# A decoder block on one core: feed-forward products as three of 256 columns, with breaks of 64-column products between them

## The chip, the core and the metric

The kernel runs on one core of a Trainium2 chip. Its time is the device time of one execution in microseconds (us). The kernel before took 2075.42, 2079.7 and 2075.45 us in three runs, a median of 2075.45 us.

## What is computed

A decoder block over 256 tokens of width 2048, in float32: a SwiGLU feed-forward of width 5632, a token mixer (8 heads of a gated delta rule and 16 heads of a state space model that share one input and one output projection), a second feed-forward, and a gated embedding with a last normalisation.

```python
h = h + 0.5 * swiglu(rmsnorm(h, ffn1_norm), ffn1_w_gate, ffn1_w_up, ffn1_w_down)
proj = rmsnorm(h, mix_norm) @ w_in
...
h = h + jnp.concatenate([o_gdn, o_ssm], axis=-1) @ w_out
h = h + 0.5 * swiglu(rmsnorm(h, ffn2_norm), ffn2_w_gate, ffn2_w_up, ffn2_w_down)
gate = jax.nn.sigmoid(rmsnorm(h, ple_norm) @ ple_w_gate)
h = h + gate * rmsnorm(p @ ple_w_proj, ple_post_norm)
return rmsnorm(h, final_norm)
```

## The kernel before

Everything is kept transposed: 128 channels on the partitions, the 256 tokens as columns. Nearly all of the work is weight tiles of 128 x 128 times an operand of 256 columns. To keep float32 accuracy both sides are split into two parts, hi (rounded) and lo (the rest): a weight tile w and an operand slice x give hi(w) hi(x), hi(w) lo(x) and lo(w) hi(x). The split operands lie in SBUF as `xs` (the block's state, 16 slices), `hid` (half of the feed-forward's hidden width, 22 slices) and `osp` (the mixer's output, 16 slices); each slice has its hi and its lo half side by side, 512 columns. The weights come by SP's queue into `raw`; for each piece of 1024 columns (8 slices) ScalarE casts `hi` (L118) and VectorE subtracts `lo` (L119).

A step is one weight tile with one slice. There are two ways to take it. `chain` (L122 to L133) multiplies hi(w) with hi and lo of the slice in one product of 512 columns into both halves of a PSUM bank (L130), and lo(w) with the hi half in a product of 256 columns into the first half (L128, or L132 in the first step). The bank's halves are added when the tile is done: `total_of` copies one half out by ScalarE (L168) and adds the other by VectorE (L169). `single` (L135 to L149) takes three products of 256 columns, all into the first half (L145 to L147), and its caller reads that half alone.

`product` uses `chain`: all gate, up and down tiles of both feed-forwards (`ffn`, from L318 on; per feed-forward two halves of 22 gate and 22 up tiles with `xs`, then 16 down tiles with `hid`), the first two tiles of the mixer's input projection, and all but the last tile of the embedding's gate. `embed` calls `chain` itself with `psp`. `single` serves the rest of the input projection, the output projection with `osp`, and the last tile.

`stats` makes the row of a normalisation: products of one column (L240) and, after VectorE and GpSimd, two products of 128 columns that spread the row over the partitions (L249), which `use` then reads. It and `embed` and the mixer's heads are generators: `tick`, called after each piece of a tile, advances each of them by one part, so their small products stand in between the big ones. The order within an engine is that of a scheduler with a simulated timeline.

The PSUM tiles `mm` (four banks) hold tiles of products; `mx_bank` gives one of four other banks for the small products. `ones` is a 128 x 128 tile of ones.

Of the kernel before, what the change touches and what calls it, by code (L numbers as in the profile page):

```python
# [12 lines left out]
ALU = mybir.AluOpType  # L13
# [37 lines left out]
STEP = 3  # L51
WARM = 11
AHEAD = 0


def constant_pack():
# [12 lines left out]
def tile_hybrid_block(ctx, tc, xT, pT, con, par, wgu1, wd1, wnar, win, wout, wgu2, wd2, wproj, wple, outT):  # L69
    nc = tc.nc  # L70
    act, dve, pool, pe = nc.scalar, nc.vector, nc.gpsimd, nc.tensor
# [14 lines left out]
    ones = cp.tile([P, P], F32, name="ones")  # L86
# [17 lines left out]
    def mx_bank(name):  # L104
        return psx.tile([P, 512], F32, tag="mx", name=name)
# [16 lines left out]
    def chain(ps, hi, lo, act_in, ks, first=True, last=True):  # L122


        for i, (w, k) in enumerate(ks):
            start, stop = first and i == 0, last and i == len(ks) - 1
            if not start:
                pe.matmul(ps[:, 0, :], lo[:, w, :], act_in[:, k, 0, :], start=False, stop=False,  # L128
                          skip_group_check=True)
            pe.matmul(ps, hi[:, w, :], act_in[:, k], start=start, stop=stop, skip_group_check=True)  # L130
            if start:
                pe.matmul(ps[:, 0, :], lo[:, w, :], act_in[:, k, 0, :], start=False, stop=False,  # L132
                          skip_group_check=True)  # L133

    def single(src, act_in, ks):  # L135

# [29 lines left out]

    def total_of(ps, out):
        act.copy(out, ps[:, 0, :])  # L168
        dve.tensor_tensor(out=out, in0=out, in1=ps[:, 1, :], op=ALU.add)  # L169


    side = []
# [1 line left out]
    def tick():  # L174
        for g in list(side):
            with tc.high_priority(offset=AHEAD):
                if next(g, g) is g:
# [53 lines left out]
    def stats(squares, width, name, use, wait=2):  # L231


        for _ in range(wait):
            yield
        m = small.tile([P, 2], F32, tag="rm", name=name + "m")
        banks = [mx_bank(f"{name}{c}") for c in range(2)]
        for i, sq in enumerate(squares):
            for c, ps in enumerate(banks):
                pe.matmul(ps[:, 0:1], sq[:, c * P:(c + 1) * P], ones[:, 0:1], start=i == 0,  # L240
                          stop=i == len(squares) - 1)
        for c, ps in enumerate(banks):
            dve.tensor_scalar(m[:, c:c + 1], ps[:, 0:1], 1.0 / width, EPS, op0=ALU.mult, op1=ALU.add)
        y = rsq(m, 2, name)
        if wait:
            yield
        ps = mx_bank(name + "row")
        for c in range(2):
            pe.matmul(ps[:, c * P:(c + 1) * P], y[:, c:c + 1].to_broadcast([P, P]), ident, start=True, stop=True)  # L249
        use(ps[:, :T])  # L250

    def begin(gen):
        side.append(gen)
        return gen
# [5 lines left out]
    def new_acc():  # L260
        return tp.tile([P, 2, T], F32, tag="acc", name="acc")
# [10 lines left out]
    ps = mx_bank("warm")  # L272
# [35 lines left out]
    def token_stats(use):  # L308

        acc = new_acc()  # L310
        for k in range(0, KD, 4):
            yield
            for i in (k, k + 2):
                sumsq(acc, hT[:, i:i + 2, :], i == 0)
        yield from stats(fold(acc), D, "ffn", use)


    def ffn(wgu, wd, squares, next_name, start=None):  # L318

        with tc.tile_pool(name="hid", bufs=1) as hp, tc.tile_pool(name="ft", bufs=2) as ft:  # L320
            hid = hp.tile([P, HF, 2, T], F32R, name="hid")
            r = hp.tile([P, T], F32, name="r")
            rh = hp.tile([P, T], F32, name="rh")
            new = new_acc()

            def use(row):
                dve.tensor_copy(r, row)
                act.mul(rh, row, 0.5)

            gen, held = None, []  # L330
            for half in range(2):
                for f in range(0, HF, 2):
                    t = ft.tile([P, 2, T], F32, tag="t", name="t")
                    s = ft.tile([P, 2, T], F32, tag="s", name="s")
                    tiles = [(wgu[half * HF + f + j, b], out[:, j, :]) for j in range(2) for b, out in ((0, t), (1, s))]
                    if start is not None:
                        start([out for _, out in tiles[:3]])
                        tiles = tiles[3:]
                        start = None
                    for n, (w, out) in enumerate(tiles):  # L340
                        if gen is None and (n == len(tiles) - 2 or len(tiles) == 1):
                            gen = begin(stats(squares(), D, "ffn", use) if squares else token_stats(use))
                        product([w], xs, full, out)
                    held.append((f, t, s))

                    if len(held) == 1 and squares is None and half == 0 and f == 0:
                        continue
                    drain([gen])
                    for g, t, s in held:
                        dve.tensor_tensor(out=t, in0=t, in1=over(r, 2), op=ALU.mult)  # L350
                        act.activation(t, t, AF.Silu)
                        dve.tensor_tensor(out=s, in0=s, in1=t, op=ALU.mult)
                        split_into(hid[:, g:g + 2], s)
                    held.clear()
                for o in range(0, KD, 2):
                    t = ft.tile([P, 2, T], F32, tag="t", name="t")
                    for j in range(2):
                        product([wd[half, o + j, q] for q in range(2)], hid, list(range(HF)), t[:, j, :])
                    dve.tensor_tensor(out=t, in0=t, in1=over(rh, 2), op=ALU.mult)
                    dve.tensor_tensor(out=hT[:, o:o + 2, :], in0=hT[:, o:o + 2, :], in1=t, op=ALU.add)  # L360
                    if half == 1:
                        split_x(o, next_name)
                        split_x(o + 1, next_name)
                        sumsq(new, hT[:, o:o + 2, :], o == 0)
        return new
# [5 lines left out]
    with ExitStack() as mix:  # L371
# [34 lines left out]
        ps = mm_bank("nar")  # L406
# [498 lines left out]
        op = mix.enter_context(tc.tile_pool(name="op", bufs=1))  # L905
# [8 lines left out]

        acc2 = new_acc()
        order = list(range(8, 16)) + list(range(8))
        for o in range(0, KD, 2):
            for j in range(2):
                ps = single(wout[o + j], osp, order)
                dve.tensor_tensor(out=hT[:, o + j, :], in0=hT[:, o + j, :], in1=ps, op=ALU.add)  # L920
            split_x(o, "ffn2")
            split_x(o + 1, "ffn2")
            sumsq(acc2, hT[:, o:o + 2, :], o == 0)
# [30 lines left out]
    with tc.tile_pool(name="f2", bufs=2) as f2:  # L954
# [29 lines left out]
            act.mul(pp[:, o, :], hT[:, o, :], pv("final")[:, o:o + 1])  # L984

        for o in range(0, KD, 2):
            last = o == KD - 2
            t = f2.tile([P, 2, T], F32, tag="t", name="t")
            for j, n in ((0, 1), (1, 1)) if last else ((0, 2),):
# [117 lines left out]
```

## Time and profile before

| | |
|---|---|
| median of three runs | 2075.45 us |
| the profiled execution's own time | 2079.58 us |
| span of its instructions | 2077.7 us |
| mean granted TensorE clock | 0.995 of full speed |
| TensorE products busy | 2051.2 us, 99%, 12882 products |
| VectorE busy | 1366.0 us, 66% |
| ScalarE busy | 1034.8 us, 50% |
| GpSimd busy | 175.3 us, 8% |
| DMA | 384.58 MB, mean 185 GB/s |

Matmuls are pipelined: a product's time in the profile runs from its start to a modelled end, and the next one starts before that. So the pace is read from start to start, in the timeline, or from the number of products in a window. A float32 product of the small kind (operands that aren't split) shows as two records in the profile.

### The profile page before, as it was taken

Reading aid. Unit: us, or ns where it says so; the run is one execution under the profiler, and the core shown is the slowest. Engines: PE = TensorE matmul, PEld = TensorE weight load, DVE = VectorE, ACT = ScalarE, POOL = GpSimd, SP = SyncE. Lnnn points to the kernel's source line nnn. Section 1 sums busy time; section 2 is a strip of 40 time slices with the busy share of each in tenths; the row PEclk is TensorE's granted clock in tenths of the full one; section 3 lists DMA queues with packets and bytes.
Section 4 is the critical chain, followed back from the end, with each engine's and each line's share of the span. In section 5 each row is a group of like instructions: output and inputs, shape, how many; then the busy total and the mean of one; then the engine's idle time right before and its main releaser. Section 6 shows DMA issues by size and latency. Waiting matters only on the chain.

```text
span 2077.7 us, 31523 instructions
## 1 busy us (share of the span) xinstructions
PE 2051.2 (99%) x12882; PEld 1835.2 (88%) x12882; DVE 1366.0 (66%) x2063; ACT 1034.8 (50%) x1544; POOL 175.3 (8%) x206
## 2 busy tenths in 40 slices
PE   9999999999999999989999999999999999999997
PEld 7888888888888889989999998888888888888886
DVE  7665555556555669999887666556555565556675
ACT  6544444444444555645545456444444444445554
POOL 2000000000000013303321111000000000000011
PEclk9999999999999999999999999999999999999998
DMA  7555455655555666544444555555556555545652
GB/s 271 185 183 185 176 176 187 210 184 188 193 173 179 203 223 205 184 160 164 174 165 161 190 183 184 193 191 183 163 186 211 190 183 183 186 164 189 210 183 102
DMA packets 64481, 384.58 MB, mean 185 GB/s; under 512 B 7744, under 2 KB 9280, under 8 KB 31184
## 3 DMA queue, kind: packets, MB, share of 16 engines
q1 hardware_dynamic: 61600, 376.76, 52.6%
q0 software_dynamic: 2448, 5.28, 0.8%
q8 instruction: 101, 1.65, 0.3%
q10 hardware_dynamic: 288, 0.52, 0.1%
q14 instruction: 44, 0.36, 0.0%
HBM read 377.78 MB, written 4.75 MB: 184 GB/s over the span
## 4 chain that ended last, share of the span: by engine, by line
PE 91%; DVE 2%; DMA 2%; issue 2%; POOL 1%; ACT 1%; POOLq 0%; DVEq 0%; ACTq 0%; SPq 0%
PE mm L130 50%; PE mm L128 24%; PE mm L146 4%; PE mm L147 4%; PE mm L145 4%; PE mm L132 1%; DMA hT<-rows 1%; DVE lo L119 1%; DMA blky<-Z 1%; DMA Y<-blky 1%; PE ip L694 0%; PE pj L130 0%; DVE u L566 0%; PE iy L694 0%; POOL hT L829 0%
## 5 line engine op out<-in xcount | busy, mean ns | idle before, releaser
L119 DVE TENSOR_TENSOR lo<-raw,hi 128x1024 fp32r<-128x1024 f32 (+1 forms) x774 | 858.5, 1117 | 482.6 <-ACT hi L118 481.8
L130 PE MATMUL mm<-xs,hi 128*128 128x512 f32 x3088 | 1078.2, 397 | 0.0
L118 ACT CAST hi<-raw 128x1024 fp32r<-128x1024 f32 (+1 forms) x774 | 744.4, 963 | 567.9 <-PE mm L130 372.7
L128 PE MATMUL mm<-xs,lo 128*128 128x256 f32 x2895 | 812.8, 281 | 3.2 <-DVE lo L119 3.2
L130 PEld LDWEIGHTS mm<-xs,hi 128*128 128x128 f32 x3088 | 568.2, 188 | 123.2 <-ACT hi L118 0.3
L128 PEld LDWEIGHTS mm<-xs,lo 128*128 128x128 f32 x2895 | 543.6, 188 | 14.8 <-DVE lo L119 4.9
L130 PE MATMUL mm<-hid,hi 128*128 128x512 f32 x1408 | 492.5, 397 | 0.0
L128 PE MATMUL mm<-hid,lo 128*128 128x256 f32 x1344 | 377.8, 281 | 0.0
L130 PEld LDWEIGHTS mm<-hid,hi 128*128 128x128 f32 x1408 | 260.2, 188 | 59.0
L128 PEld LDWEIGHTS mm<-hid,lo 128*128 128x128 f32 x1344 | 253.3, 188 | 3.0
L147 PE MATMUL mm<-xs,lo 128*128 128x256 f32 x816 | 229.9, 282 | 4.3 <-DVE lo L119 4.3
L145 PE MATMUL mm<-xs,hi 128*128 128x256 f32 x816 | 230.1, 282 | 0.0
L146 PE MATMUL mm<-xs,hi 128*128 128x256 f32 x816 | 229.5, 281 | 0.0
L147 PEld LDWEIGHTS mm<-xs,lo 128*128 128x128 f32 x816 | 154.9, 190 | 5.0 <-DVE lo L119 4.9
L146 PEld LDWEIGHTS mm<-xs,hi 128*128 128x128 f32 x816 | 154.9, 190 | 0.4
L145 PEld LDWEIGHTS mm<-xs,hi 128*128 128x128 f32 x816 | 154.7, 190 | 0.6 <-issue 0.3
L168 ACT COPY t<-mm 128x256 f32<-128x256 f32 x167 | 62.3, 373 | 161.9 <-PE mm L130 160.7
L205 POOL TENSOR_TENSOR acc<-acc,sq 128x512 f32<-128x512 f32 x43 | 63.1, 1467 | 944.8 <-ACT sq L204 906.3
L169 DVE TENSOR_TENSOR t<-t,mm 128x256 f32<-128x256 f32 x167 | 69.9, 418 | 86.9 <-ACT t L168 86.8
L168 ACT COPY s<-mm 128x256 f32<-128x256 f32 x88 | 32.8, 373 | 149.0 <-PE mm L130 148.9
L169 DVE TENSOR_TENSOR s<-s,mm 128x256 f32<-128x256 f32 x88 | 37.1, 422 | 74.0 <-ACT s L168 73.9
L147 PE MATMUL mm<-osp,lo 128*128 128x256 f32 x256 | 71.8, 281 | 0.0
(303 smaller groups left out, 1452.8 us busy)
## 6 DMA issues: line engine op xcount, KB each, us to landing
raw<-in_wgu SPq DMA_DIRECT2D x173, 1024.0 KB, 4.8
raw<-in_wd SPq DMA_DIRECT2D x128, 704.0 KB, 4.1
raw<-in_win SPq DMA_DIRECT2D x52, 1024.0 KB, 4.8
raw<-in_wout SPq DMA_DIRECT2D x16, 1024.0 KB, 4.8
raw<-in_wple SPq DMA_DIRECT2D x16, 1024.0 KB, 4.8
first<-in_wgu SPq DMA_DIRECT2D x11, 256.0 KB, 6.7
hold<-hT POOLq DMA_DIRECT2D x4, 512.0 KB, 4.0
Lb<-blkl SPq DMA_DIRECT2D x4, 512.0 KB, 4.6
```

Of the source, the lines that this page charges most:

```text
L118: act.copy(hi, src)
L119: dve.tensor_tensor(out=lo, in0=src, in1=hi.bitcast(F32), op=ALU.subtract)
L128: pe.matmul(ps[:, 0, :], lo[:, w, :], act_in[:, k, 0, :], start=False, stop=False, skip_group_check=True)
L130: pe.matmul(ps, hi[:, w, :], act_in[:, k], start=start, stop=stop, skip_group_check=True)
L132: pe.matmul(ps[:, 0, :], lo[:, w, :], act_in[:, k, 0, :], start=False, stop=False, skip_group_check=True)
L145: pe.matmul(ps[:, 0, :], hi[:, i, :], act_in[:, k, 0, :], start=k == ks[0], stop=False)
L146: pe.matmul(ps[:, 0, :], hi[:, i, :], act_in[:, k, 1, :], start=False, stop=False)
L147: pe.matmul(ps[:, 0, :], lo[:, i, :], act_in[:, k, 0, :], start=False, stop=k == ks[-1])
L168: act.copy(out, ps[:, 0, :])
L169: dve.tensor_tensor(out=out, in0=out, in1=ps[:, 1, :], op=ALU.add)
L205: pool.tensor_tensor(out=acc, in0=acc, in1=sq, op=ALU.add)
```

## The change

`chain` now takes a step as `single` does, in three products of 256 columns into the bank's first half, and `total_of` only copies that half. A new function `pause` issues four products of 64 columns, float32, ones times ones, into columns 256 to 319 of a bank; nobody reads them. It is called in `stats` behind the row's products (not for the last row), in both feed-forwards ahead of every fourth pair of gate and up tiles (f = 4, 12, 20 of each half), ahead of the down tiles and in the middle of them, ahead of the output projection, and ahead of the third pair of embedding gate tiles.

```diff
+PAUSE = 4
+WIDTH = 64
...
         for i, (w, k) in enumerate(ks):
             start, stop = first and i == 0, last and i == len(ks) - 1
-            if not start:
-                pe.matmul(ps[:, 0, :], lo[:, w, :], act_in[:, k, 0, :], start=False, stop=False,
-                          skip_group_check=True)
-            pe.matmul(ps, hi[:, w, :], act_in[:, k], start=start, stop=stop, skip_group_check=True)
-            if start:
-                pe.matmul(ps[:, 0, :], lo[:, w, :], act_in[:, k, 0, :], start=False, stop=False,
-                          skip_group_check=True)
+            pe.matmul(ps[:, 0, :], hi[:, w, :], act_in[:, k, 0, :], start=start, stop=False)
+            pe.matmul(ps[:, 0, :], hi[:, w, :], act_in[:, k, 1, :], start=False, stop=False)
+            pe.matmul(ps[:, 0, :], lo[:, w, :], act_in[:, k, 0, :], start=False, stop=stop)
+
+    def pause(ps):
+
+        for i in range(PAUSE):
+            pe.matmul(ps[:, 256:256 + WIDTH], ones, ones[:, 0:WIDTH], start=True, stop=True)
...
     def total_of(ps, out):
         act.copy(out, ps[:, 0, :])
-        dve.tensor_tensor(out=out, in0=out, in1=ps[:, 1, :], op=ALU.add)
...
             pe.matmul(ps[:, c * P:(c + 1) * P], y[:, c:c + 1].to_broadcast([P, P]), ident, start=True, stop=True)
+        if wait:
+            pause(ps)
         use(ps[:, :T])
...
                 for f in range(0, HF, 2):
+                    if f % 8 == 4:
+                        pause(mx_bank("calm"))
...
+                pause(mx_bank("calm"))
                 for o in range(0, KD, 2):
+                    if o == 8:
+                        pause(mx_bank("calm"))
...
         order = list(range(8, 16)) + list(range(8))
+        pause(mx_bank("calm"))
         for o in range(0, KD, 2):
...
         for o in range(0, KD, 2):
+            if o == 4:
+                pause(mx_bank("calm"))
```

TensorE's order where the first feed-forward goes from its last up tile (`xs`) to its first down tile (`hid`), before and after; the numbers behind the names tell one buffer from the next:

```order
L128 MATMUL mm_2243<-xs_80,lo_2267 128x256
L130 MATMUL mm_2243<-xs_80,hi_2266 128x512
L130 MATMUL mm_2294<-hid_111,hi_2297 128x512
L132 MATMUL mm_2294<-hid_111,lo_2298 128x256
L128 MATMUL mm_2294<-hid_111,lo_2298 128x256
```

```order
L129 MATMUL mm_2907<-xs_80,hi_2938 128x256
L130 MATMUL mm_2907<-xs_80,hi_2938 128x256
L131 MATMUL mm_2907<-xs_80,lo_2939 128x256
L136 MATMUL calm_2972<-ones_83 128x64 x4
L129 MATMUL mm_2978<-hid_111,hi_2981 128x256
L130 MATMUL mm_2978<-hid_111,hi_2981 128x256
L131 MATMUL mm_2978<-hid_111,lo_2982 128x256
```

Two products to a step have become three, and the break stands between the two kinds of tiles, where the source has it.

TensorE's order where the mixer's last projection tile (`xs`) is followed by the first tile of the output projection (`osp`), before and after:

```order
L145 MATMUL mm_11236<-xs_80,hi_11267 128x256
L146 MATMUL mm_11236<-xs_80,hi_11267 128x256
L147 MATMUL mm_11236<-xs_80,lo_11268 128x256
L145 MATMUL mm_11302<-osp_11159,hi_11305 128x256
L146 MATMUL mm_11302<-osp_11159,hi_11305 128x256
L147 MATMUL mm_11302<-osp_11159,lo_11306 128x256
```

```order
L148 MATMUL mm_13324<-xs_80,hi_13355 128x256
L149 MATMUL mm_13324<-xs_80,hi_13355 128x256
L150 MATMUL mm_13324<-xs_80,lo_13356 128x256
L136 MATMUL calm_13390<-ones_83 128x64 x4
L148 MATMUL mm_13395<-osp_13247,hi_13398 128x256
L149 MATMUL mm_13395<-osp_13247,hi_13398 128x256
L150 MATMUL mm_13395<-osp_13247,lo_13399 128x256
```

The products of `single` are the same as before, three lines further down; the break is all that is new there.

## Rows read from the trace of the kernel before

**Rows 1.** The page: TensorE's busy time, and the granted clock in 40 slices

```profile
PE 2051.2 (99%) x12882; PEld 1835.2 (88%) x12882; DVE 1366.0 (66%) x2063; ACT 1034.8 (50%) x1544; POOL 175.3 (8%) x206
...
PEclk9999999999999999999999999999999999999998
```

**Rows 2.** The page's costly groups: count, busy us, mean ns; idle before, releaser

```profile
L130 PE MATMUL mm<-xs,hi 128*128 128x512 f32 x3088 | 1078.2, 397 | 0.0
...
L128 PE MATMUL mm<-xs,lo 128*128 128x256 f32 x2895 | 812.8, 281 | 3.2 <-DVE lo L119 3.2
...
L130 PE MATMUL mm<-hid,hi 128*128 128x512 f32 x1408 | 492.5, 397 | 0.0
...
L147 PE MATMUL mm<-xs,lo 128*128 128x256 f32 x816 | 229.9, 282 | 4.3 <-DVE lo L119 4.3
...
L169 DVE TENSOR_TENSOR t<-t,mm 128x256 f32<-128x256 f32 x167 | 69.9, 418 | 86.9 <-ACT t L168 86.8
...
L169 DVE TENSOR_TENSOR s<-s,mm 128x256 f32<-128x256 f32 x88 | 37.1, 422 | 74.0 <-ACT s L168 73.9
```

**Rows 3.** TensorE's timeline, an up tile: start us, duration us

```profile
200.08 0.40 PE L130 MATMUL mm<-xs,hi 128*128 128x512 f32 x1
...
203.26 0.40 PE L130 MATMUL mm<-xs,hi 128*128 128x512 f32 x1
```

**Rows 4.** TensorE's timeline, a down tile

```profile
1901.63 0.40 PE L130 MATMUL mm<-hid,hi 128*128 128x512 f32 x1
...
1905.86 0.39 PE L130 MATMUL mm<-hid,hi 128*128 128x512 f32 x1
```

**Rows 5.** Windows of TensorE: us, busy us (count), granted clock, DMA share, GB/s

```profile
783.10:806.50 23.40, 23.40 (x209) 1.00 0.56 196
...
1125.00:1205.00 80.00, 80.00 (x679) 1.00 0.55 190
```

**Rows 6.** TensorE's timeline, the kernel's last tile and what follows it

```profile
2057.38 0.28 PE L145 MATMUL mm<-xs,hi 128*128 128x256 f32 x1
...
2063.03 0.50 PE L240 MATMUL final<-ones,acc 128*128 128x1 f32 x4
```

**Rows 7.** TensorE's timeline around the mixer's row of statistics

```profile
777.29 0.60 PE L249 MATMUL mixrow<-cont,mix 128*128 128x128 f32 x4
...
778.21 0.28 PE L146 MATMUL mm<-xs,hi 128*128 128x256 f32 x1
...
779.15 0.28 PE L145 MATMUL mm<-xs,hi 128*128 128x256 f32 x1
```

**Rows 8.** TensorE's timeline around four 64-column products in the mixer

```profile
924.25 1.00 PE L694 MATMUL ip<-oT,LA 128*128 128x64 f32 x8
925.06 0.36 PE L145 MATMUL mm<-xs,hi 128*128 128x256 f32 x1
...
926.19 0.28 PE L145 MATMUL mm<-xs,hi 128*128 128x256 f32 x1
...
928.57 0.28 PE L145 MATMUL mm<-xs,hi 128*128 128x256 f32 x1
```

**Rows 9.** TensorE's timeline behind other 64-column products

```profile
1082.42 1.06 PE L694 MATMUL iy<-Y,blockQ 128*128 128x64 f32 x8
...
1083.84 0.28 PE L145 MATMUL mm<-xs,hi 128*128 128x256 f32 x1
...
1084.20 0.28 PE L145 MATMUL mm<-xs,hi 128*128 128x256 f32 x1
```

**Rows 10.** TensorE's timeline from the mixer's last projection tile into the output projection

```profile
1123.00 0.28 PE L147 MATMUL mm<-xs,lo 128*128 128x256 f32 x1
...
1123.45 0.28 PE L145 MATMUL mm<-osp,hi 128*128 128x256 f32 x1
...
1124.39 0.28 PE L147 MATMUL mm<-osp,lo 128*128 128x256 f32 x1
```

**Rows 11.** A window of all engines: PE, PEld, DVE, ACT, POOL, granted clock, DMA

```profile
900.00:950.00 50.00, 46.48 (x374) 45.88 (x373) 43.91 (x128) 22.24 (x40) 8.79 (x15) 0.93 0.45 155
```

## The prediction

> **What bounds the kernel now.** I read the page first: TensorE is busy for 99% of the span at the full granted clock [rows 1], so the time is TensorE's instruction stream and little else. The table of costly groups says what the stream is: products of 512 and 256 columns by the thousand, with next to no idle time in front of them: the lo products with xs waited 3.2 us in total in `chain`, and 4.3 in `single` [rows 2]. VectorE, ScalarE and the DMA rows are cover: what the change takes from them is worth nothing by itself. So the question is at what pace TensorE goes through its columns, and for that I went to the timeline and to windows.
>
> There are two paces at the same granted clock. A feed-forward step of `chain` (512 and 256 columns) with xs goes from 200.08 to 203.26 us in nine steps: 353.3 ns a step, or 117.8 ns for 256 columns [rows 3]. With hid it is 12 steps in 4.23 us, 352.5 ns, 117.5 for 256 columns [rows 4]. In the mixer, `single` does the same step as three products of 256, and there 783.10 to 806.50 holds 209 of them; each is 0.28 us long, so two or three of the count only reach in, and 23.40 us over 206.5 is 113.3 ns. The output projection, the same instructions with osp, took 80 us for 679 less the same 2.5: 118.3 ns [rows 5]. The last tile of the kernel, three products with xs behind a `chain`, took 5.65 us for 48: 117.7 ns [rows 6]. So three products instead of two are no faster as such. Some stretches run at 113.3 and others at 117.5 to 118.3, and I call the two paces fast and slow.
>
> What changes the pace is another kind of product in between. Behind the two 128-column products of the mixer's row of statistics, the fast pace became slow: 779.15 less 778.21 is 0.94 us for eight [rows 7]. Behind four 64-column products (two records each, eight in the row) it is fast: from 926.19 to 928.57 stand 21 products, 113.3 ns each [rows 8]. There are four such breaks in the mixer, and all four left it fast; two had found it slow. Once, behind sixteen mixed records of 64 columns, it was slow afterwards: 1083.84 to 1084.20 is 0.36 for three [rows 9]. Without a break I find no product with xs at which the fast pace was lost.
>
> **The change part by part.** (a) `chain` becomes three products of 256. By rows 3 and 6 this costs nothing in the slow pace with xs (353.3 against 3 x 117.7 = 353.1). It is what makes the feed-forward stream the same as the one that ran fast. There are 3088 steps with xs and 1408 with hid [rows 2].
>
> (b) The 255 VectorE adds of `total_of` go (69.9 + 37.1 us, [rows 2]). TensorE, ACT and the queues wait for none of them where it counts: the products behind them had no idle time. I take 0; at the drained ends of a stage it could give back some tenths of a microsecond.
>
> (c) The breaks. The built order has 29 of them, each four 64-column products, where the source puts them. The nearest row is the one of the mixer: from 924.25 to 926.19 there are a break and nine steps at 113.3 (1.02 us), which leaves 0.92 us for the break [rows 8]. Its eight records alone are 0.81 (924.25 to 925.06), the floor. A ceiling of 1.0 allows for more settling. 29 x 0.92 = 26.7 us, all on the path, since TensorE has nothing else that waits; between 23.5 and 29. Of their waits the built order has only ones for TensorE's own earlier products (the break before in that bank), so nothing new holds up the products queued behind. Where a break sits behind a row of statistics (seven of the 29) VectorE's reading of the row comes up to 0.9 us later, and TensorE has a tile of products in front of the next thing that needs it.
>
> (d) The fast pace where it is reached. Counted in the built order, 7765 products with xs follow a break with no hid or osp in between (354 stand ahead of the first break). At 117.8 - 113.3 = 4.5 ns each that is -34.9 us. The other 1223 products with xs come behind hid or osp without a break; the nearest row, the last tile, says that a slow stream stays slow, so 0, with -5.5 as the other bound.
>
> (e) The products with hid: 4224 of them, each run behind a break, and 768 with osp. The trace has no break ahead of hid or osp. What it has is the entry: the fast pace of xs (1123.00 to 1123.45, four in 0.45) turned slow at the very first product with osp, with no idle time, and the next eight took 0.94 us [rows 10]; it stayed there for 80 us [rows 5]. I read this as belonging to the operand and take slow, at the pace of osp since that is the same instruction: (118.3 - 117.5) x 4224 = +3.4 us. Bounds: 0, and if they go fast like xs, -4.2 x 4224 = -17.7, and osp -5.0 x 768 = -3.8.
>
> The sum: 26.7 - 34.9 + 3.4 = -4.8 us. The profiled execution took 2079.58 us (span 2077.7 and 1.9 around it), so it would be 2074.8 there. That execution lies 4.1 over the median of the three runs, 2075.45, two of which agree at 2075.4; on the median it is **2070.6 us**, 0.23% less.
>
> The Trainium skill ("TensorE: Matmul & The Clock Gate", section on the back-to-back issue gap) gives a warm product N/2.4 GHz plus about 2.5 ns, fixed. By that rule a third product per step costs 4496 x 2.5 = 11.2 us, an estimate from that page, and speaks against (a). The sum would then be 2081.8 us. With xs the trace doesn't agree: 512 and 256 columns took 353.3 ns and three of 256 took 353.1 [rows 3, 6], and neither pace is the page's 109 ns for 256 columns.
>
> **The rivals.**
> 1. *hid and osp go fast too.* For it: the break sets the pace in every stretch where I can see one, and neither operand ever had a break ahead of it, so one entry from xs is thin evidence. Against: that entry, without any stall. Then 26.7 - 34.9 - 17.7 - 3.8 - 5.5 = -35.2: 2040.2 us.
> 2. *The fast pace doesn't last in the feed-forward.* The longest stretch that I can lean on is some 206 products [rows 5]; here nine runs with xs have 576 to 768 products between breaks, beside DMAs, casts and subtractions for every 24. If it is lost after 206, only 2899 of the 7765 run fast, 13.0 us, and 26.7 + 3.4 - 13.0 = +17.1: 2092.6 us, slower. It decides from the length at which the gain covers 30.1 us: 6690 products, about 627 in each long run. Against it: the stalls in the mixer (4.3 us in front of `single`'s lo products, [rows 2]) left fast products behind them.
> 3. *The breaks don't set the pace here*, as in rows 7 and 9, where products of 64 or 128 columns left it slow; then the change is its price alone, +30.1: 2105.6 us. For it: each of those breaks had other operands than a break here, and with a fixed rhythm one bad outcome would repeat at all 29 places. Against: the nearest form left it fast four times of four.
> 4. *The third product of a step costs its own time in the feed-forward.* With osp three products of the slow pace take 3 x 118.3 = 354.9 ns, with hid two take 352.5 [rows 4, 5]. If the 2.4 ns are the third product's and not osp's, as (e) has it for hid, the 3088 steps with xs pay them too: +7.4 us, 2078.0 us. Against it: rows 3 and 6, where xs shows no such difference.
>
> Beside these the mixer's order shifts a little, and its dip in the granted clock (0.93 over the 50 us from 900, which at half clock is 7 us at half speed, 3.5 us lost, [rows 11]) may move, go or get a second: 3.5 us up or down, which I put into the range of the forecast.
>
> **How the numbers follow.** Chances: forecast 0.48, hid and osp fast 0.27, fast pace lost 0.14, breaks without effect 0.08, a price for the third product 0.03. The forecast's own range is -34.9 + 23.5 - 5.5 = -16.9 to -34.9 + 29 + 3.4 = -2.5, with 3.5 for the dip: 2055 to 2077. A measurement of this kernel can tell about 0.2%, 4.2 us, from no change, so the line for faster is at 2071.3. In the forecast's case I give 0.70 to faster, 0.25 to the same and 0.05 to slower. Faster: 0.27 + 0.34 = 0.61; the same: 0.12, and 0.03 for rival 2 where the pace lasts about 600 products: 0.15; slower: 0.24. The range goes down to rival 1 with the floor price of the breaks (2040.2 - 3.2 = 2037, with a little of the dip: 2036) and up to rival 2 (2093); rival 3 is left out.
>
> **What would show it.** In the profile after, a window between two breaks of the gate and up tiles has 113.3 ns for each product (100 us hold 883 of them, where slow gives 849), and the down tiles about 118. A break's eight records take 0.8 us. If windows of the down tiles show 113, rival 1 is right and the time is near 2040. If the count falls from 883 to 849 within a run, rival 2 is right; if the window right behind a break has 849, rival 3. The forecast is wrong in its cause, whatever the time, if the pace changes at places that aren't breaks or changes of operand.

## The result, and the profile after

The changed kernel took 2106.99 us (median of four runs, 2103.44 to 2110.08) against 2076.89 beside it: 1.45% slower, the ratio of the times is 1.0145 with a 95% interval of 1.0132 to 1.0158. The forecast was 2070.6 with a range of 2036 to 2093, so the sign was wrong and the time lies outside the range. It is the time of rival 3, 2105.6. The profiled execution took 2105.64 us (span 2103.8), 26.1 more than that of before; the medians differ by 30.1, since that execution of before lies 2.7 us over the median beside it and that of after 1.4 under its own.

The page of the changed kernel, TensorE's line and the granted clock in 40 slices, answers to [rows 1]:

```profile
PE 2076.6 (99%) x17642; PEld 2068.6 (98%) x17642; DVE 1256.5 (60%) x1790; ACT 1026.2 (49%) x1544; POOL 172.7 (8%) x206
...
PEclk9999999999999999999999999999999999999998
```

TensorE is as full as before, at the same clock. VectorE lost its adds (1366.0 to 1256.5 us) and nothing came of it. The costly groups, for [rows 2] (count, busy us and mean ns of one; idle time before):

```profile
L131 PE MATMUL mm<-xs,lo 128*128 128x256 f32 x3088 | 865.3, 280 | 2.7 <-DVE lo L121 2.6
L129 PE MATMUL mm<-xs,hi 128*128 128x256 f32 x3088 | 867.0, 281 | 0.6 <-ACT hi L120 0.6
...
L131 PE MATMUL mm<-hid,lo 128*128 128x256 f32 x1408 | 395.5, 281 | 0.0
```

Still no idle time in front of them, so what is longer is longer by TensorE's own pace and by more products. Windows of TensorE alone (from:to in us; length, busy time and count, granted clock, DMA share, GB/s) show the pace, as [rows 5] did:

```profile
60.00:140.00 80.00, 80.00 (x682) 1.00 0.53 185
270.00:320.00 50.00, 50.00 (x425) 1.00 0.58 187
395.00:430.00 35.00, 35.00 (x312) 1.00 0.57 201
440.00:520.00 80.00, 80.00 (x681) 1.00 0.53 185
1620.00:1660.00 40.00, 40.00 (x355) 1.00 0.55 198
1670.00:1750.00 80.00, 80.00 (x682) 1.00 0.53 185
```

Some 2.4 products of each count only reach in. 80 us hold 682 products with xs: 117.7 ns each, the slow pace (fast would be 708). hid has 118.3 (425 in 50 us). Of these only 395 to 430 and 1620 to 1660 are fast, 113.1 and 113.4 ns: there xs comes behind hid *without* a break. The break at 433.62 ends it, in TensorE's timeline (start us, duration us):

```profile
432.82 0.28 PE L131 MATMUL mm<-xs,lo 128*128 128x256 f32 x1
...
433.50 0.28 PE L131 MATMUL mm<-xs,lo 128*128 128x256 f32 x1
433.62 1.00 PE L136 MATMUL calm<-ones 128*128 128x64 f32 x8
434.42 0.36 PE L129 MATMUL mm<-xs,hi 128*128 128x256 f32 x1
434.62 0.28 PE L130 MATMUL mm<-xs,hi 128*128 128x256 f32 x1
...
435.56 0.28 PE L129 MATMUL mm<-xs,hi 128*128 128x256 f32 x1
```

Six products in 0.68 us before it (113 ns), eight in 0.94 behind it (117.5). The break's eight records take 0.80 us. In the mixer, the row that the forecast leaned on [rows 8] still reads as before:

```profile
936.53 1.00 PE L703 MATMUL ip<-oT,LA 128*128 128x64 f32 x8
937.34 0.36 PE L148 MATMUL mm<-xs,hi 128*128 128x256 f32 x1
...
938.01 0.28 PE L150 MATMUL mm<-xs,lo 128*128 128x256 f32 x1
...
940.05 0.28 PE L150 MATMUL mm<-xs,lo 128*128 128x256 f32 x1
```

Eighteen products in 2.04 us, 113.3 ns: this break leaves the fast pace, the change's does not, and in the profile both are eight records of 64 columns in 0.81 us.

By stage (from the first product of one kind in the timeline to that of the next, profiled executions, us; 1 and 2 are the feed-forwards, a and b their halves):

| | xs 1a | hid 1a | xs 1b | hid 1b | mixer | osp | xs 2a | hid 2a | xs 2b | hid 2b | embedding |
|---|---|---|---|---|---|---|---|---|---|---|---|
| before | 254.2 | 124.2 | 248.2 | 124.2 | 366.7 | 90.9 | 260.2 | 124.2 | 248.2 | 124.2 | 97.2 |
| after | 258.4 | 125.9 | 250.6 | 125.9 | 369.9 | 91.0 | 265.2 | 125.9 | 250.6 | 125.9 | 99.2 |
| e1, no breaks | 254.2 | 125.0 | 239.4 | 125.0 | 372.8 | 90.9 | 260.4 | 125.0 | 239.4 | 125.0 | 94.0 |
| e8, and place | 246.2 | 119.7 | 239.4 | 119.7 | 376.5 | 90.5 | 252.2 | 119.7 | 239.4 | 119.7 | 96.5 |

After lies above before in every stage, and the differences make up the 26.1 us.

### The profile page after: what moved, and what is told of

Read it like the earlier page. It is cut to its first block, busy times and chain, and to the rows that moved or that the text cites. A ratio compares the mean times of both kernels' runs of the same rounds, so it can differ in the third digit from the quotient of the medians.

```text
span 2103.8 us, 41216 instructions
## 1 busy us (share of the span) xinstructions
PE 2076.6 (99%) x17642; PEld 2068.6 (98%) x17642; DVE 1256.5 (60%) x1790; ACT 1026.2 (49%) x1544; POOL 172.7 (8%) x206
## 4 chain that ended last, share of the span: by engine, by line
PE 93%; DMA 2%; issue 2%; DVE 2%; POOL 1%; ACT 1%; SPq 0%; POOLq 0%; DVEq 0%; ACTq 0%
PE mm L129 25%; PE mm L131 25%; PE mm L130 25%; PE mm L148 5%; PE mm L149 5%; PE mm L150 5%; PE calm L136 1%; DMA hT<-rows 1%; DVE lo L121 1%; PE ip L703 0%; DMA blkl<-LA 0%; DMA hT<-in_xT 0%; PE iy L703 0%; DMA blky<-Z 0%; POOL hT L838 0%
## 5 line engine op out<-in xcount | busy, mean ns | idle before, releaser
L131 PE MATMUL mm<-xs,lo 128*128 128x256 f32 x3088 | 865.3, 280 | 2.7 <-DVE lo L121 2.6
L129 PE MATMUL mm<-xs,hi 128*128 128x256 f32 x3088 | 867.0, 281 | 0.6 <-ACT hi L120 0.6
L130 PE MATMUL mm<-xs,hi 128*128 128x256 f32 x3088 | 865.1, 280 | 0.0
L131 PEld LDWEIGHTS mm<-xs,lo 128*128 128x128 f32 x3088 | 587.2, 190 | 3.7 <-DVE lo L121 3.7
L130 PEld LDWEIGHTS mm<-xs,hi 128*128 128x128 f32 x3088 | 583.1, 189 | 0.0
L129 PEld LDWEIGHTS mm<-xs,hi 128*128 128x128 f32 x3088 | 579.8, 188 | 1.2 <-ACT hi L120 1.2
L129 PE MATMUL mm<-hid,hi 128*128 128x256 f32 x1408 | 396.2, 281 | 0.0
L130 PE MATMUL mm<-hid,hi 128*128 128x256 f32 x1408 | 395.6, 281 | 0.0
L131 PE MATMUL mm<-hid,lo 128*128 128x256 f32 x1408 | 395.5, 281 | 0.0
L130 PEld LDWEIGHTS mm<-hid,hi 128*128 128x128 f32 x1408 | 265.3, 188 | 0.0
L129 PEld LDWEIGHTS mm<-hid,hi 128*128 128x128 f32 x1408 | 265.3, 188 | 0.0
L131 PEld LDWEIGHTS mm<-hid,lo 128*128 128x128 f32 x1408 | 265.3, 188 | 0.0
L150 PE MATMUL mm<-xs,lo 128*128 128x256 f32 x816 | 230.0, 282 | 5.5 <-DVE lo L121 5.5
L148 PE MATMUL mm<-xs,hi 128*128 128x256 f32 x816 | 230.9, 283 | 1.0 <-ACT hi L120 1.0
L149 PE MATMUL mm<-xs,hi 128*128 128x256 f32 x816 | 229.6, 281 | 0.0
L150 PEld LDWEIGHTS mm<-xs,lo 128*128 128x128 f32 x816 | 155.1, 190 | 6.2 <-DVE lo L121 6.1
L148 PEld LDWEIGHTS mm<-xs,hi 128*128 128x128 f32 x816 | 154.9, 190 | 2.0 <-ACT hi L120 1.4
L149 PEld LDWEIGHTS mm<-xs,hi 128*128 128x128 f32 x816 | 155.1, 190 | 0.3
```

The source lines that it names most:

```text
L129: pe.matmul(ps[:, 0, :], hi[:, w, :], act_in[:, k, 0, :], start=start, stop=False)
L130: pe.matmul(ps[:, 0, :], hi[:, w, :], act_in[:, k, 1, :], start=False, stop=False)
L148: pe.matmul(ps[:, 0, :], hi[:, i, :], act_in[:, k, 0, :], start=k == ks[0], stop=False)
L149: pe.matmul(ps[:, 0, :], hi[:, i, :], act_in[:, k, 1, :], start=False, stop=False)
L150: pe.matmul(ps[:, 0, :], lo[:, i, :], act_in[:, k, 0, :], start=False, stop=k == ks[-1])
```

## The experiments

The ratios are to the kernel before, run beside them, with 95% intervals. "Place" is the byte in its partition, modulo 256, at which a tile starts in the built program: 128 for xs and `ones`, 192 for the weights hi and lo, 160 for hid, osp, the mixer's oT and the embedding's psp, 224 for the mixer's LA (of [rows 8], where oT is the moving operand and LA the weights).

| run | median us | ratio, interval |
|---|---|---|
| e1, three products, no breaks | 2067.72 | 0.9957, 0.9942 to 0.9971 |
| e2, the kernel before with the breaks | 2103.35 | 1.0123, 1.0106 to 1.0140 |
| e3, e1 with hid and osp at 192 | 2074.83 | 0.9987, 0.9978 to 0.9996 |
| e4, after with hid and osp at 192 | 2119.58 | 1.0202, 1.0187 to 1.0217 |
| e5, e1 with hid and osp at 0 | 2067.99 | 0.9976, 0.9955 to 0.9998 |
| e6, e1 with xs at 160, weights at 64, hid at 32 | 2115.15 | 1.0191, 1.0174 to 1.0208 |
| e8, e1 with hid and osp at 128 | 2037.39 | 0.9808, 0.9794 to 0.9823 |
| e9, e8 and two breaks of one product | 2031.28 | 0.9787, 0.9768 to 0.9805 |
| e10, before with hid and osp at 128 | 2074.64 | 0.9987, 0.9978 to 0.9996 |
| e11, after with hid and osp at 128 | 2111.28 | 1.0174, 1.0157 to 1.0191 |
| e13, after, other weights in the breaks | 2082.58 | 1.0028, 1.0019 to 1.0038 |
| e14, e8 and two breaks with other weights | 2029.50 | 0.9769, 0.9753 to 0.9786 |
| e15, e11, other weights in the breaks | 2052.45 | 0.9880, 0.9866 to 0.9895 |

### One part alone: e1 and e2

e1 is the changed kernel without a break; e2 is the kernel before with all of them.

```diff
-        if wait:
-            pause(ps)
...
-                    if f % 8 == 4:
-                        pause(mx_bank("calm"))
```

(and the other calls likewise; e2 adds the same lines to the kernel before). Expected of e1:

> The changed kernel with its 29 breaks left out: three products of 256 columns alone. Theory A (a break's cost is its own 0.92 us, and behind most breaks of the feed-forward the stream went on in the slow pace of 117.8 ns, also where it had run at 113.3 ahead of the break): the 26.7 us of the breaks go, the runs with xs that were fast until a break ended them (from 386 and from 1614 us of the changed kernel) stay fast for the whole second half of each feed-forward, some 4200 products at 4.5 ns, 19 us; the time is 2107 - 27 - 19 + a few = about 2060 us, under the kernel before. Theory B (the third product costs time of its own, and the breaks at least do no harm to the pace): 2107 - 27 = 2080 us or more, and the second halves fall back to 117.8 without any break.

and of e2:

> The kernel before with the 29 breaks alone; a step stays at 512 and 256 columns. Theory A: the pace of 353 ns a step has no fast form with 512 columns, so the time is the price of the breaks, 0.92 us each: 2076.9 + 27 = 2104 us. Theory B (most of the loss is the third product): clearly less, 2085 to 2095 us.

e2 is 26.3 us above before, 0.91 us for each of 29 breaks (0.76 to 1.00 by the interval), and its gate and up tiles keep their pace. Its breaks don't all stand where after has them: in its trace the first down tiles of each feed-forward hold the five `calm` breaks of the second half too, most of them in pieces, and the second half has none. So e2 gives the price of 29 breaks, but not at these 29 places. e1 is 9.3 us *below* before. Windows of TensorE in e1:

```profile
60.00:140.00 80.00, 80.00 (x681) 1.00 0.53 187
...
405.00:600.00 195.00, 195.00 (x1723) 1.00 0.55 195
...
1620.00:1800.00 180.00, 180.00 (x1591) 1.00 0.56 195
```

195 us hold 1723: 113.3 ns, the fast pace, through a whole half with no break in it; the first halves (681 in 80) are slow. So three products can run fast by themselves, and the change's breaks cost their 26.3 us and the fast stretches too. Part of e1's gain is given back in its mixer, which is 6.1 us longer than before (the table). The 37.8 us between the profiled executions of e1 and after come out of these parts: 26.3 for the breaks, 18.0 for some 4000 fewer fast products (counted as below, 4.5 ns each), less the 6.5 us by which e1's mixer is longer than after's without its four breaks. All engines of e1 in the mixer's worst 50 us (TensorE, weight loads, VectorE, ScalarE, GpSimd; clock; DMA):

```profile
1000.00:1050.00 50.00, 40.23 (x328) 38.10 (x327) 41.06 (x127) 19.96 (x45) 19.27 (x31) 0.86 0.40 132
```

and what TensorE waited for in that mixer (total us, times, longest):

```profile
PE ip L696 <- DVE oT L685: 9.1, 2, 7.6
```

TensorE waits 7.6 us for VectorE's oT, against 3.5 at the longest before, is busy for 40.23 of the 50 us, and the granted clock of the stretch is 0.86. Before has its dips elsewhere, 0.93 in the 50 us from 900 [rows 11] and 0.97 in those from 1000; e1 has a second one of 0.97 in those from 800. That is 8.5 us lost to the clock in e1's mixer for 5.0 in that of before, in one execution of each. Why the wait became longer no run here takes apart.

### Where the operands stand: e3 to e6

A tile of 32 or 96 bytes in a pool of its own moves hid and osp. In e6 one of 32 bytes ahead of xs and one of 96 behind it move xs by 32 bytes and all that follows by 128.

```diff
+    padp = ctx.enter_context(tc.tile_pool(name="padp", bufs=1))
...
+    pool.memset(padp.tile([P, 8], F32, name="pad"), 0.0)
```

Expected of e3, e4, e5 and e6:

> No breaks, three products, and a tile of 32 bytes per partition put ahead of the pools of hid and osp, so that these begin at a multiple of 64 bytes as xs does (before, 32 over one). Theory A with the operand's place as the reason why hid and osp are slow: their products can run at 113.3 ns too, (118.3 - 113.3) x 4992 = 25 us less than without breaks alone where they all do: about 2035 us. Rival (they are slow for another reason: the size, the neighbours, what VectorE and ScalarE do meanwhile): the same time as without breaks alone, and 118 ns in the down tiles.

> The changed kernel with its breaks, and hid and osp moved by 32 bytes per partition. Theory A: the breaks put the stream into the slow pace as in the changed kernel, now in the same regular form for hid and osp (117.8 instead of 118.2): 2105 us, at most 2 us under the changed kernel. Rival (the break sets the fast pace and only the operand's place kept hid and osp from it): their 4992 products at 113.3, 2080 us.

> No breaks, three products, hid and osp moved by 96 bytes per partition, so that their first byte stands at 0 of 128 as that of xs does (xs 0, weights hi and lo 64; hid and osp 32 before, 64 in the run that moved them by 32 and where they took 120.0 ns). Theory C (the pace depends on where the streamed operand starts against 128 bytes, or against the weights): the down tiles and the output projection now run as xs does, 113.3 or 117.7 ns and never 118.2 or 120; where the fast pace of xs is carried in, 4992 x 5 = 25 us less than 2068: 2043 us, and 2065 if all of them are slow. Rival (the operand's size or its neighbours): 118 or 120 as before, 2068 us or more.

> The mirror: no breaks, three products, xs moved by 32 bytes so that it starts at 32 of 128 as hid and osp do; everything behind it moved by 128, which leaves their places as they were. Theory C: no product with xs at 113.3 in the feed-forwards any more, all at about 118.2; what the run without breaks won there is gone: 2077 + 3 and some of the mixer's fast stretches: 2085 to 2095 us. Rival (xs is fast for another reason): 2068 us.

Windows in hid's stage, e3 (hid at 192) and then e5 (hid at 0):

```profile
260.00:310.00 50.00, 50.00 (x419) 1.00 0.54 181
```

```profile
260.00:310.00 50.00, 50.00 (x427) 1.00 0.56 188
```

419 less 2.4 is 120.0 ns, 427 is 117.8, against 118.3 at 160: the pace of the same instruction hangs on the place of its operand. At none of the three was a stretch with hid fast. In e6 xs never ran at 113.3; its windows with xs and with hid:

```profile
60.00:140.00 80.00, 80.00 (x669) 1.00 0.52 185
270.00:320.00 50.00, 50.00 (x425) 1.00 0.55 183
```

120.0 and 118.3 ns. By the operand's own place this doesn't fit (160 has 118.3 with hid in e1, 120.0 with xs here), by its distance from the weights modulo 256 all rows do: -64 (xs in e1) has 113.3 or 117.8, +64 (hid in e5) 117.8, -32 (hid in e1 and in e6) 118.3, 0 (e3) and +96 (xs in e6) 120.0. Only e6 moved the weights, so that reading rests on one kernel. That all of xs ran at 120.0 there, and not at the 118.2 expected, is most of why e6 took 2115.15 and not 2085 to 2095. e4 lies 44.8 us above e3, for the breaks' price and the fast stretches of xs again, with hid at 120.0.

### Is four products of 64 the right break? e7

Twelve breaks of other kinds at the places of the gate and up tiles, in e1; one run, 2079.87 us.

```diff
+    KINDS = [(1, 64), (2, 64), (3, 64), (5, 64), (4, 32), (4, 48), (4, 96), (4, 128), (2, 128), (6, 64), (1, 128), (1, 32)]
```

> No breaks but twelve, at the places among the gate and up tiles where the changed kernel has them, each of another kind (number of products x columns, in order: 1x64, 2x64, 3x64, 5x64, 4x32, 4x48, 4x96, 4x128, 2x128, 6x64, 1x128, 1x32). Theory D (a break sets the pace by the moment at which it lets the stream go on, and that moment is the same for one kind): some kinds leave the pace at 113.3 and others at 117.7, whatever it was ahead of them. Rival (any break among these tiles ends in the slow pace, since a new tile begins behind it): slow behind all twelve.

Products of 256 columns in 20 us behind each (179 is fast, 172 slow): behind one and three of 64, four of 32 and one of 128 the slow stream became fast; behind two, five and six of 64 and four of 48 the fast one became slow; four and two of 128 left it slow, one of 32 left it fast. Four of 96 stand where products with psp come in between, and say nothing. So a break can give the fast pace, but not by its number of products or columns in any order that I can read.

### hid where xs stands: e8 to e11

```diff
+    pool.memset(padp.tile([P, 56], F32, name="pad"), 0.0)
```

in e1 (e8), in the kernel before (e10) and in the changed one (e11); e9 is e8 with one product of 64 columns ahead of the output projection and one in the embedding.

> As the run with hid and osp moved by 96 bytes, but by 224, so that they start at 128 of 256 as xs does. If 128 bytes are what counts: the same paces as there. If 256: 113.3 or 117.7 here and something else there.

> The fastest so far (no breaks, hid and osp moved by 224 bytes, 2037.4 us) with two short breaks of one 64-column product each, the kind that took a slow stream to 113.3 three times of three: ahead of the output projection and ahead of the third pair of embedding gate tiles. There the stream ran at 117.8 for 768 and some 550 products. Theory D: both go to 113.3, 1300 x 4.5 = 5.9 us less and 0.5 us for the breaks: 2032 us. Rival (the kind's effect doesn't carry over to another place): 2038 us.

> The kernel before with hid and osp moved by 224 bytes and nothing else. Theory: with 512 columns in a step there is no pace of 113.3 to be had, so the feed-forwards stay at 353 ns a step; at most the output projection gains (768 x 5 = 3.8 us): 2073 to 2077 us. Rival (the place alone brings it): 2050 us or less.

> The changed kernel, breaks and all, with hid and osp moved by 224 bytes. Theory: a break of four 64-column products ends in the slow pace among these tiles wherever the operand stands, so hid goes from 118.2 to 117.8 only, and xs and hid are slow behind each break: 2103 to 2107 us. Rival (the breaks do no more than cost their 0.92 us): 2037 + 27 = 2064 us.

Windows in e8 (xs, hid, osp):

```profile
60.00:140.00 80.00, 80.00 (x708) 1.00 0.55 196
258.00:308.00 50.00, 50.00 (x443) 1.00 0.58 194
...
1130.00:1200.00 70.00, 70.00 (x597) 1.00 0.52 185
```

and in e11 (xs, hid):

```profile
65.00:145.00 80.00, 80.00 (x682) 1.00 0.53 185
270.00:320.00 50.00, 50.00 (x427) 1.00 0.57 188
```

In e8 both feed-forwards run at 113.4 ns throughout, hid too (443 in 50 us), and the pace passes from xs to hid and back. In e11 the breaks hold both at 117.7 to 117.8. With 512 columns the place gives nothing in the feed-forwards (e10, whose gain is osp's: 87.0 us for 90.9). So the place of the operand allows the fast pace, the breaks take it, and they take it even where everything else is right for it. In e9 the break in the embedding turned slow into fast (487 products in 55 us), the one ahead of osp fast into slow. So its median, 0.7 us from the 2032 expected with both fast, doesn't bear that expectation out; its profiled execution, the slowest of four, lies 1.0 us above that of e8.

### The break's own weights: e12, e13, e15, e14

e12 is e8 with twelve breaks of four 64-column products whose two operands come from `ones` (at 128) or from a second tile of ones at 160, where oT stands in the kernel before.

```diff
+    pad = padp.tile([P, 248], F32, name="pad")
+    pool.memset(pad, 1.0)
+    off = pad[:, SHIFT:SHIFT + P]
...
-            pe.matmul(ps[:, 256:256 + WIDTH], ones, ones[:, 0:WIDTH], start=True, stop=True)
+            pe.matmul(ps[:, 256:256 + WIDTH], w, m[:, 0:WIDTH], start=True, stop=True)
```

> The kernel without the change's breaks, its hidden and out-projection tiles 224 bytes on as in e8, with twelve breaks of four 64-column products inside the gate/up stages of both layers (behind tiles 4, 12 and 20 of each half), whose weights and moving operand are ones tiles at two places: one as the change has it (called ones, 128 of 256) and one 32 bytes on (called off, 160 of 256, where the attention's tile stands in the kernel before). Pairs (weights, moving) in order of the breaks: off/off, off/off, ones/ones, off/off, ones/off, off/ones, ones/off, off/off, off/off, off/ones, off/off, ones/ones. Theory that the place of the break's own operands decides: all five off/off breaks leave the stream at 113.3 ns and both ones/ones at 117.8, with the mixed pairs like one of the two. Rival, that it hangs on the moment at which the stream starts again and on the pace ahead of the break: the same pair leaves both paces at different places. Nothing else of the kernel changes; the time is that of e8 (2037.4) plus 12 x 0.91 = 10.9 us, plus 4.5 ns for every product that a break leaves slow.

(There are six off/off breaks in that list.) Time 2063.72, one run. Windows of TensorE behind the first six breaks, off/off, off/off, ones/ones, off/off, ones/off and off/ones (weights/moving):

```profile
58.00:78.00 20.00, 20.00 (x179) 1.00 0.49 168
147.00:167.00 20.00, 20.00 (x179) 1.00 0.53 190
234.00:254.00 20.00, 20.00 (x172) 1.00 0.40 131
428.00:448.00 20.00, 20.00 (x179) 1.00 0.53 186
516.00:536.00 20.00, 20.00 (x172) 1.00 0.50 176
607.00:627.00 20.00, 20.00 (x179) 1.00 0.43 146
```

Fast behind all eight breaks with weights at 160 (three had found it slow), slow behind all four with weights at 128 (each had found it fast), whatever the moving operand. The other three runs put only this into known kernels: weights at 160, moving operand `ones`. The second tile also moves what lies behind it, in e13 by 1024 bytes and in e14 and e15 by 992, which leaves each place modulo 256 as it was in after, e8 and e11.

```diff
-            pe.matmul(ps[:, 256:256 + WIDTH], ones, ones[:, 0:WIDTH], start=True, stop=True)
+            pe.matmul(ps[:, 256:256 + WIDTH], off, ones[:, 0:WIDTH], start=True, stop=True)
```

> The changed kernel with all its 29 breaks, in which only the weights of the breaks are another tile of ones, which starts at 160 of 256 (bytes) where `ones` starts at 128; their moving operand stays `ones`, and all other tiles keep their place within 256. Theory that the place of the break's own weights decides at which pace it leaves the stream: behind the breaks of the gate and up tiles xs runs at 113.3 ns where it ran at 117.8 in the changed kernel. Of the 7765 products with xs behind a break some 800 were fast already (one stretch, 1282 to 1377 us), so 6960 x 4.5 ns = 31 us come back: 2107.0 - 31 = 2076 us. hid and osp stay at 118.2. Rival, that the fast outcomes in the run before (e12) came from that kernel's moved tiles or places: xs stays at 117.8 behind most breaks, 2107 us.

> The same with the hidden and out-projection tiles at 128 of 256, as in e11 (e11 and these weights of the breaks). Theory: every product of the feed-forwards with xs and hid, the output projection and the embedding's gate at 113.3 behind each break. From e8 (2037.4), whose feed-forwards were fast throughout: 29 x 0.91 = 26.4 us for the breaks, -3.4 us for the 768 products with osp, -3 us for the embedding's gate: 2057 us. Rival as before: slow behind the breaks, as e11, 2111 us.

> e8 (no break of the change, hidden and out-projection tiles at 128 of 256) with two breaks of four 64-column products whose weights start at 160 of 256, ahead of the output projection and ahead of the embedding gate's third pair. Theory of the break's weights: both leave the stream fast, osp 113.3 instead of 117.8 (768 x 4.5 = 3.4 us) and the embedding's gate likewise (some 640 x 4.5 = 2.9 us), less 2 x 0.91: 2037.4 - 4.5 = 2033 us. Rival: slow behind them as behind the output projection's break in e9: 2039 us.

Windows of e13 (xs, hid, xs, the exception, xs):

```profile
60.00:140.00 80.00, 80.00 (x708) 1.00 0.56 194
260.00:310.00 50.00, 50.00 (x424) 1.00 0.52 176
430.00:510.00 80.00, 80.00 (x709) 1.00 0.54 191
1275.00:1360.00 85.00, 85.00 (x723) 1.00 0.52 186
1370.00:1450.00 80.00, 80.00 (x709) 1.00 0.53 187
```

of e15 (xs, hid, osp):

```profile
60.00:140.00 80.00, 80.00 (x709) 1.00 0.53 189
260.00:310.00 50.00, 50.00 (x444) 1.00 0.56 187
...
1120.00:1220.00 100.00, 100.00 (x885) 1.00 0.54 191
```

In e13 eleven of the twelve breaks among gate and up tiles leave the stream fast, where in after none does for more than 3 us; its time is 24.4 us below after, of 31 expected. The count agrees: some 7050 products with xs are fast for some 1400 in after, 25.4 us, and the profiled executions differ by 26.3. The expectation had kept the fast stretches behind hid, and they are gone in e13 (768 products, 3.5 us). The break that left it slow, ahead of 1275, stands among products with psp, which is at 160; the 800 products behind it, which the expectation took for fast in after, were slow there too but for the first 3 us. In e15, where psp is at 128 as well, all 12 are fast, all 8 of hid and the one of osp.

The breaks behind a row of statistics don't follow this. The first of them, among the first gate and up tiles, left the stream slow in e13 and e15, with weights at 160, and fast in e11, with weights at 128 (21 products from 54.70 to 57.08, 113.3 ns). Behind e13's, at 52.74:

```profile
54.11 0.28 PE L134 MATMUL mm<-xs,hi 128*128 128x256 f32 x1
...
56.93 0.28 PE L134 MATMUL mm<-xs,hi 128*128 128x256 f32 x1
```

24 products in 2.82 us, 117.5. So the place of the weights decides for four products of 64 that come straight behind a product with xs or hid, and not for those behind a row's products or psp.

The 32 bytes of one operand of a product that nobody reads are worth 24 us of 2107, and 59 of 2111. e14 is the best version: 47.5 us, 2.3%, below the kernel before.

## Why the prediction was wrong, point by point

The failed step is (d): "7765 products with xs follow a break with no hid or osp in between ... At 117.8 - 113.3 = 4.5 ns each that is -34.9 us". In the changed kernel some 1400 of the 9264 products with xs in `chain` were fast (counted in the trace, by the mean start-to-start time of twelve neighbours; the counts hold to some 2%), most of them in stretches that no break began. The `calm` breaks found the stream fast four times: behind three of them xs was slow, and the fourth stands ahead of osp, which is slow in e1 without it. What I took for the nearest row [rows 8] was the nearest in form, and the form doesn't decide: its weights LA stood at 224 and its moving oT at 160, where `ones` is at 128. e3 moves the two to 0 and 192 and leaves xs and its weights in place. There the break of [rows 8] found the stream fast and left it slow:

```profile
927.80 1.00 PE L698 MATMUL ip<-oT,LA 128*128 128x64 f32 x8
...
929.05 0.28 PE L150 MATMUL mm<-xs,hi 128*128 128x256 f32 x1
...
931.52 0.28 PE L150 MATMUL mm<-xs,hi 128*128 128x256 f32 x1
```

21 products in 2.47 us, 117.6 ns, for 113.3 in before. I had this doubt as rival 3 ("each of those breaks had other operands than a break here, and with a fixed rhythm one bad outcome would repeat at all 29 places"), gave it 0.08 and left it out of the range. Four breaks that agreed were one break four times.

The same step was wrong once more, the other way. It gave the products behind hid 0, because [rows 6] shows a slow stream that stays slow. They ran fast (395 to 430 us above). In e1 that grows to whole halves, some 5400 fast products without any break of the change. So breaks weren't needed for the fast pace, and what I said of breaks as that which changes the pace was drawn from a kernel whose feed-forwards had no stream of three products.

- (a), three products for two at no cost: nearly, but mis-sized. [rows 3] takes a step from nine, with starts to 0.01 us. Over the long stretch from 60 to 250 us, before and then e1:

```profile
60.49 0.40 PE L130 MATMUL mm<-xs,hi 128*128 128x512 f32 x1
...
249.78 0.40 PE L130 MATMUL mm<-xs,hi 128*128 128x512 f32 x1
```

```profile
60.30 0.28 PE L129 MATMUL mm<-xs,hi 128*128 128x256 f32 x1
...
249.68 0.28 PE L129 MATMUL mm<-xs,hi 128*128 128x256 f32 x1
```

Here 537 steps of before took 352.5 ns each and 536 slow steps of e1 353.3. So three products cost 0.8 ns a step more than two with xs, 2.6 us over 3088 steps, where the sum had nothing. The Trainium skill's fixed 2.5 ns for each product ("TensorE: Matmul & The Clock Gate", section on the back-to-back issue gap, which gives it for an isolated product) would add 11.2 us, an estimate from that page. The trace has a third of it for each step.

- (b), VectorE's adds: right, nothing came back.
- (c), the price of a break: right, for 0.92 said 0.91 us each in e2, and 0.88 at the change's own places, where the second half's gate and up tiles are fast throughout: 242.9 us with four breaks in e15, 239.4 without in e8 (xs 1b).
- (e), hid and osp slow: right in the number, 118.3 and +0.8 us in each of four stages (125.0 for 124.2 in e1), 3.2 for 3.4 said. Its reading, that this belongs to the operand, holds for the operand's place only: at 128 the same hid runs at 113.4 (e8).
- Rival 1 is a real mechanism: e15 has it, at 2052.45, with the place and the break's weights mended. Rival 2 is not: with no break in it the fast pace lasted 195 us and more (e1). Rival 4 has a third of its size, 2.6 of 7.4 us, by (a); at 2078.0 us it also lies within the 4.2 us of no change, so its 0.03 was put under slower by mistake.
- Rival 3 has the time, and in part by luck. Its ground, other operands, is what the runs show; but it has them leave the pace as it is, and they set it, to slow. What adds up to the 26.1 us of the profiled executions is 26.3 for the breaks, 3.2 for hid and 2.6 for (a), less 6.3 for the 1400 fast products: 25.8.

In the forecast's own terms e13 is close to the change that I had predicted: some 7050 fast products at 4.5 ns are -31.7, the breaks +26.3, hid +3.2 and (a) +2.6, together +0.4 for -4.8 said. Its profiled execution lies 0.2 below that of before, its median 5.6 above: that execution of before lies 2.6 over the 2076.97 of these runs, and e13's, the fastest of ten, 3.2 under its own median. So also with the break's weights mended the change isn't faster than before; what is faster leaves the change's breaks out (e1, e8, e14) or has hid at 128 as well (e15).

## What to carry to other kernels

A pace seen behind an instruction belongs to that instruction with its operands where they stand; before a term of the sum is multiplied by thousands, look whether the row that gives it shares the addresses too, not only the shape. When several rows agree, ask whether they are independent or one case repeated, and keep the case in the range where they don't carry over. And put the parts of a change on the chip apart: here one half gained 9 us and the other lost 39.

## What the runs showed of the hardware

At a granted clock of 1.00, products of 256 columns went at 113.3 ns or at one of three slower paces, 117.7 to 117.8, 118.3 and 120.0, and stayed at it for hundreds of microseconds. With the weights at 192 of 256 bytes, hid at 128, 0, 160 and 192 had 113.4 or 117.8, 117.8, 118.3 and 120.0; only at 128 was the fast pace ever seen, for hid as for xs, and e6 speaks for the distance between the two as what counts. Which of the two a stream at 128 takes is set by what came before it, such as a small product and the place of its weights (e12, e13, e15; not behind rows of statistics), and then kept: 1723 products in 195 us without a change. A few products with psp at 160 among them ended a fast stretch in the changed kernel, 3 us behind the break at 1282.21. A step of 512 and 256 columns took 352.5 ns, three products of 256 340.0 (113.3 each) or 353.3. Why the places work so is not shown by any run here; nor is the rule for the breaks of e7. And the pace is not free downstream: e8's feed-forwards are 51.6 us shorter than before, its mixer 9.8 us longer.
